# A hybrid decoder layer on one core: the last two value tiles of the attention go to other PSUM banks, and their last weight unit goes ahead of the first scores

## The chip, the cores and the metric

The kernel runs on one core of one Trainium2 chip. The metric is the device time of one execution in microseconds (us), the median of the runs shown. Besides those runs there is one execution under the hardware profiler, from which every row below comes.

The engines are named as in the profile: PE is TensorE (matmuls), PEld its weight loads, DVE VectorE, ACT ScalarE, POOL GpSimd, SP the engine that issues most transfers. Each works through its own instructions in their order.

## What is computed

One layer of a decoder for 512 tokens of width 1024, in float32:

```
u = RMSNorm(x);  z = u @ w_in          # q, k, v of attention | q, k, v, gates of an mLSTM | two branch gates
A = block-sparse causal attention      # 8 heads of 64, rotary on q and k, blocks of 256
B = chunked mLSTM                      # 4 heads of 128
m = sigmoid(gA) * (A @ w_proj_a) + sigmoid(gB) * (B @ w_proj_b)
x = x + m @ w_out
x = x + (silu(u2 @ w_gate) * (u2 @ w_up)) @ w_down,  u2 = RMSNorm(x);  then a last RMSNorm
```

The change touches only `z`'s columns for the attention's values (512 tokens by 512 columns, `va`) and what stands beside them in the program.

## The kernel before, in words

**Arithmetic.** Every float32 operand is split into a high and a low part (`split_hl`, line 157: ACT copies the high part, line 148; DVE subtracts it, line 161), and a product is three matmuls: high by high, low by high, high by low.

**Weight units.** The weights of the first half come in 60 units of 128x1024 float32, in the order of `UNITS` (line 68): q and k (six units), then `va` 0 to 3, then k 2 and 3, the output gate `ob` 0 and 1, and so on. `fill` (line 356) works off the next unit: it first splits units up to two ahead (`LOOK`), then calls the unit's generator up to its `yield`, calls `mid` if it was given one, and lets the generator finish. `split_unit` (line 189) takes two buffers of the kind W for each unit. There are ten of these; two are held by the parts of `u` for k 2 and 3 until all projections are done. The four `va` units hold the other eight until their last use, so unit 10 (k 2) can't be split before the `va` products let go of `va` 0's buffers. The raw weights go through buffers of the kind R, and the transfer of a later unit is issued on SP once a split has freed one.

**The values.** `run_v` (line 463) multiplies the four token tiles t = 0 to 3 (128 tokens each) with the four units. A unit holds two of the eight slices of the contraction. Tiles 0 and 1 are summed as the units arrive, in two banks of the kind `mm`. When the last unit is there, their sums are taken out by `evacuate` (ACT line 148 the high part, DVE line 487 the low part, two of each for a tile), and tiles 2 and 3 are multiplied in one go with all four units: 24 matmuls of 128x512 each (lines 470 to 472), in banks of the kind `mm`.

**PSUM.** Eight banks: three of the kind `mm` (all projections), three of the kind `S` (scores, transposes and the like), two of the kind `acc` (the attention's and the mLSTM's outputs, first used by `moba_c`, line 1309). A new tile of a kind waits until the bank that it takes has been read.

**The order of the work.** Up to `man.close()` the order is written out by hand. After it, a list scheduler fixes each engine's order when the program is built: its priority is the order in the program, and an instruction that isn't ready in its own estimate of the times lets later ones pass. On the chip, each engine then keeps that order. Around the change the program runs: unit q 3, `va` 0, the first gate rows (`gate_group(0)`), `va` 1, `va` 2, the mLSTM gates (`gates`, lines 1165 to 1187, a chain on DVE that ends with line 1184 and an ACT exponential), then the main loop. Step n of that loop traces the scores of one head and half (`moba_a`: lines 1219 to 1221 for the first 256 tokens, 1244 to 1246 for the others), then `fill(1, mid)` with one weight unit, then what had been put off (`later`, lines 1192 and 1193), and, some steps later, transposes (line 1290) and the products with the values (line 1309). At step 0 the scores are those of head 0, the unit is `va` 3, and `mid` runs between this unit's products for tiles 0 and 1 and their evacuation. The scores read stacks of k (`ks1`, `ks2`) that are gathered through DRAM by eight transfers of line 424, half of them issued on SP, half on POOL.

```
while n < len(steps) or qa or qb:
    ...
    r, second = moba_a(h, b) if kind == "a" else ml_a(h, b)
    ...
    fill(1, mid)
```

The second half of the layer (from about 400 us) is the gated feed-forward part with Strassen-like block sums, its order set by priorities from a plan of due times (`at`). The change does not touch it.

Of the kernel before, what the change touches and what calls it, by code (L numbers as in the profile page):

```python
# [84 lines left out]
def hybrid_layer_kernel(ctx: ExitStack, tc, xT, wall, wgu, wds, wdl, g3v, vecs, wgates, consts, rope, out):  # L85
# [13 lines left out]
    def nm(p="t"):  # L99
        cnt[0] += 1  # L100
        return f"{p}{cnt[0]}"
# [4 lines left out]
    def slot4(dt=F32, name="f"):  # L106
        return act.tile([P, 4, S], dt, name=nm(name), tag="A4", bufs=NA4)
# [8 lines left out]
    def mmb():  # L116
        return psum.tile([P, S], F32, name=nm("mm"), tag="mm", bufs=3)
# [4 lines left out]
    def accb():  # L122
        return psum.tile([P, S], F32, name=nm("acc"), tag="acc", bufs=2)
# [22 lines left out]
    def act_(out_, in_, func, **kw):  # L146
        if func not in SETS:
            return A.activation(out_, in_, func, **kw)  # L148
        table(SETS[func])
        if ph["manual"]:  # L150
            return A.activation(out_, in_, func, **kw)
        with tc.issue_after(ph["load"]):
            i = A.activation(out_, in_, func, **kw)
        ph["ins"].append(raw_ins(i))
        return i
# [33 lines left out]
    def split_unit():  # L189
        u = wstate["split"]  # L190
        wstate["split"] += 1
        whl[u] = split_hl(raw.pop(u), dst=(blk(F32R, "wh"), blk(F32R, "wl")))
        if u % 2 == 1:
            load_pair() if u < NGEN - 4 else st["load"]()
# [143 lines left out]
    def advance(n=1):  # L338
        for _ in range(n):
            while bulk:  # L340
                try:
                    next(bulk[0])
                    break
                except StopIteration:
                    bulk.pop(0)
# [5 lines left out]
    def add(g):  # L351
        bulk.append(g)
        return g


    def fill(n=1, mid=None):

        for _ in range(n):
            u = pos[0]
            if u >= len(UNITS):  # L360
                if mid:
                    mid()
                return
            while wstate["split"] <= min(u + LOOK, NGEN - 1):
                split_unit()
            pos[0] += 1
            kind, i = UNITS[u]
            g = run[kind](i, *whl.pop(u))
            next(g, None)
            if mid:  # L370
                mid()
            for _ in g:
                pass
# [89 lines left out]
    def run_v(kind):  # L463
        def products(ps, t, units):
            c = slice(t * P, (t + 1) * P)
            for j, (wh, wl) in units:
                for e in range(2):
                    k = 2 * j + e
                    h, l = wh[:, S * e : S * e + S], wl[:, S * e : S * e + S]
                    T.matmul(ps, uh[k][:, c], h, start=k == 0, stop=False)  # L470
                    T.matmul(ps, uh[k][:, c], l, start=False, stop=False)
                    T.matmul(ps, ul[k][:, c], h, start=False, stop=k == KT - 1)

        def evacuate(ps, t):
            c = slice(t * P, (t + 1) * P)
            for j in range(2):
                d = st[kind, j]
                o = ps[:, 256 * j : 256 * j + 256]
                if kind == "va":

                    o = o.rearrange("p (h d) -> p h d", h=4)
                    h, l = d[:, :, t * P : t * P + 64], d[:, :, t * P + 64 : (t + 1) * P]
                else:
                    o = o.rearrange("p (h d) -> p h d", h=2)
                    h, l = d[:, 0:4:2, c], d[:, 1:4:2, c]
                act_(h, o, AF.Copy, scale=rt[:, t : t + 1])
                V.scalar_tensor_tensor(l, o, rt[:, t : t + 1], f(h), op0=ALU.mult, op1=ALU.subtract)

        def fn(i, wh, wl):
            if i == 0:  # L490
                st[kind] = []
                st[kind, "ps"] = [mmb(), mmb()]
                for j in range(2):
                    d = st[kind, j] = slot4(F32R, kind)
                    if kind == "vb":
                        vml[2 * j], vml[2 * j + 1] = (d[:, 0, :], d[:, 1, :]), (d[:, 2, :], d[:, 3, :])
                    for e in range(4 if kind == "va" else 0):
                        vat[4 * j + e] = d[:, e, :]
            st[kind].append((i, (wh, wl)))
            for t in range(2):  # L500
                products(st[kind, "ps"][t], t, st[kind][-1:])
            yield
            if i == 3:
                for t in range(2):
                    evacuate(st[kind, "ps"][t], t)
                for t in range(2, 4):
                    ps = mmb()
                    products(ps, t, st[kind])
                    evacuate(ps, t)
        return fn  # L510
# [767 lines left out]
    def moba_b(h, b, prs):  # L1278

        res = []  # L1280
        for half in range(b + 1):
            pt = sb()
            n = 0
            for kk in range(2):
                kt = 2 * half + kk
                for t in range(2):
                    if kt > 2 * b + t:
                        continue
                    src = prs[0][:, P * (t + kt) : P * (t + kt + 1)] if b == 0 else prs[t][:, P * kt : P * kt + P]
                    T.transpose(pt[:, n : n + P], src, ident)  # L1290
                    n += P
            h_, l_ = slot(F32R, "pth"), slot(F32R, "ptl")
            res.append(split_hl(pt[:, :n], dst=(h_[:, :n], l_[:, :n])))
        return res
# [52 lines left out]
    def ml_a(h, b):  # L1347
        qh, ql = qkm[h]
        kh, kl = qkm[4 + h]
        res = []  # L1350
        for i in ((0, 1), (2,))[b]:
            ps = mmb() if i == 1 else sb()
            w = rbc[h][i]
            n = w.shape[-1]
            for j in range(4):
                if KR[j][0] == i:
                    c = slice(j * P, (j + 1) * P)
                    o = ps[:, KR[j][1]]
                    T.matmul(o, kh[:, c], qh[:, j * P :], start=True, stop=False)
                    T.matmul(o, kl[:, c], qh[:, j * P :], start=False, stop=False)  # L1360
                    T.matmul(o, kh[:, c], ql[:, j * P :], start=False, stop=True)
            V.scalar_tensor_tensor(w, ps[:, :n], sc_b, w, op0=ALU.mult, op1=ALU.mult)
            h_, l_ = slot(F32R, "Ah"), slot(F32R, "Al")
            res.append(split_hl(w, dst=(h_[:, :n], l_[:, :n])))

        w0, w1, w2 = rbc[h][0:3]
        if b == 0:
            V.tensor_tensor(w0[:, P:], w0[:, P:], w1, op=ALU.add)
        else:
            V.tensor_tensor(w0[:, 2 * P :], w0[:, 2 * P :], w2[:, 0:256], op=ALU.add)  # L1370
            V.tensor_tensor(w0[:, 3 * P :], w0[:, 3 * P :], w2[:, 256:384], op=ALU.add)
            res.append(split_hl(w0, "D"))
        return res, lambda: None
# [52 lines left out]
    for h in range(4):  # L1426
        for b in range(2):
            steps.append(("b", h, b))

    qa, qb = [], []  # L1430
    norms, norms_out = [], {}
    n = 0
# [10 lines left out]
    while n < len(steps) or qa or qb:  # L1443
        if qa and (len(qa) >= LA or n >= len(steps)):
            kind, h, b, r = qa.pop(0)
            qb.append((kind, h, b, moba_b(h, b, r) if kind == "a" else r, n))
        if n < len(steps):
            kind, h, b = steps[n]
            while kind == "b" and not (h in wready and h in qkm and 4 + h in qkm):
                advance()  # L1450
            r, second = moba_a(h, b) if kind == "a" else ml_a(h, b)
            qa.append((kind, h, b, r))
        else:
            second = lambda: None
        fl = list(pend)
        del pend[:]

        def mid():
            if n == 5:
                gate_group(1)  # L1460
            for g in todo.pop(n, ()):
                add(g)
            advance(2 if n < 13 else 3)
            second()

        fill(1, mid)
        for p_ in fl:
            p_()
        if norms:
            add(norm_d2(*norms.pop(0)))  # L1470
        while qb and (qb[0][4] <= n - LC):
            kind, h, b, r, _ = qb.pop(0)
            if kind == "a":
                moba_c(h, b, r)
            else:
                ml_c(h, b, r)
                if b == 1:
                    norms.append((h, ml_d1(h)))
        n += 1
# [106 lines left out]
```

## Time and profile before

| | |
|---|---|
| median of 3 runs | 759.62 us (758.28 to 760.0) |
| the profiled execution, its own time | 761.87 us |
| span in its profile, first to last instruction | 760.1 us |
| PE busy | 738.9 us (97%) |
| DVE busy | 624.0 us (82%) |
| ACT busy | 429.3 us (56%) |
| mean granted clock of PE | 0.991 |

A busy share is the time in which an engine had an instruction under way. "Idle before" is the time that the engine stood still ahead of an instruction, and the arrow names what ended that wait. Where an instruction waits for several things, the profile names the one that came last by its records, which can be a bystander. Matmuls overlap: one of 128x512 is shown with 0.39 us, while the next one starts 0.23 us after it.

### The profile page before, as it was taken

Reading aid. Unit: us, or ns where it says so; the run is one execution under the profiler, and the core shown is the slowest. Engines: PE = TensorE matmul, PEld = TensorE weight load, DVE = VectorE, ACT = ScalarE, POOL = GpSimd, SP = SyncE. Lnnn points to the kernel's source line nnn. Section 1 sums busy time; section 2 is a strip of 40 time slices with the busy share of each in tenths; the row PEclk is TensorE's granted clock in tenths of the full one; section 3 lists DMA queues with packets and bytes.
Section 4 is the critical chain, followed back from the end, with each engine's and each line's share of the span. In section 5 each row is a group of like instructions: output and inputs, shape, how many; then the busy total and the mean of one; then the engine's idle time right before and its main releaser. Section 6 shows DMA issues by size and latency. Waiting matters only on the chain. (4 is left out here: it accounts for less than half of the span.)

```text
span 760.1 us, 11421 instructions
## 1 busy us (share of the span) xinstructions
PE 738.9 (97%) x4230; PEld 639.0 (84%) x4230; DVE 624.0 (82%) x1065; ACT 429.3 (56%) x739; POOL 65.6 (9%) x82
## 2 busy tenths in 40 slices
PE   9998999999999999999999999989999999999994
PEld 5786888888888888888889997989899899899983
DVE  6896875889996787567688999878989988988996
ACT  7534666568765438523456566545745655665535
POOL 0002000000000000000000001300400400130003
PEclk9999999999999999999999999999999999999998
DMA  8776562432323213433676444962993795596402
GB/s 330 249 228 168 188 194 67 139 121 77 132 102 113 84 56 111 166 112 110 174 193 175 138 126 104 253 198 78 234 256 97 186 277 148 120 261 203 166 1 111
DMA packets 50839, 118.70 MB, mean 156 GB/s; under 512 B 4944, under 2 KB 9688, under 8 KB 50784
## 3 DMA queue, kind: packets, MB, share of 16 engines
q1 hardware_dynamic: 36832, 88.82, 34.7%
q0 software_dynamic: 9440, 26.77, 17.7%
q10 hardware_dynamic: 4512, 2.39, 1.0%
q8 instruction: 33, 0.54, 0.3%
q14 instruction: 22, 0.18, 0.1%
HBM read 101.16 MB, written 16.81 MB: 155 GB/s over the span
## 5 line engine op out<-in xcount | busy, mean ns | idle before, releaser
L148 ACT ACTIVATE wh<-raw 128x1024 fp32r<-128x1024 f32 x58 | 61.2, 1058 | 69.8 <-PE mm L202 63.0
L161 DVE TENSOR_TENSOR wl<-raw,wh 128x1024 fp32r<-128x1024 f32 x58 | 70.5, 1220 | 15.3 <-ACT wh L148 12.8
L783 PE MATMUL mm<-bq,w 128*128 128x256 f32 x264 | 77.0, 292 | 3.8 <-ACT s L148 3.3
L785 PE MATMUL mm<-bq,w 128*128 128x256 f32 x264 | 75.1, 284 | 0.0
L784 PE MATMUL mm<-bq,w 128*128 128x256 f32 x264 | 75.0, 284 | 0.0
L148 ACT ACTIVATE w<-s 128x1024 fp32r<-128x1024 f32 x44 | 46.6, 1060 | 45.7 <-DVE s L740 17.2
L731 DVE TENSOR_TENSOR w<-s,w 128x1024 fp32r<-128x1024 f32 x44 | 53.8, 1222 | 17.6 <-ACT w L148 15.8
L783 PEld LDWEIGHTS mm<-bq,w 128*128 128x128 f32 x264 | 50.7, 192 | 7.7 <-ACT s L148 5.4
L693 POOL DMA_DIRECT2D s<-in_wgu_dram x22 | 19.4, 882 | 413.8 <-DVE ga L585 127.8
L201 PE MATMUL mm<-u,wh 128*128 128x512 f32 x136 | 54.9, 403 | 0.0
L203 PE MATMUL mm<-u,wh 128*128 128x512 f32 x136 | 53.2, 391 | 0.0
L202 PE MATMUL mm<-u,wl 128*128 128x512 f32 x136 | 53.1, 390 | 0.0
L203 PE MATMUL mm<-ul,wh 128*128 128x512 f32 x136 | 52.9, 389 | 0.0
L201 PE MATMUL mm<-uh,wh 128*128 128x512 f32 x136 | 52.9, 389 | 0.0
L202 PE MATMUL mm<-uh,wl 128*128 128x512 f32 x136 | 52.9, 389 | 0.0
L148 ACT ACTIVATE w<-raw 128x1024 fp32r<-128x1024 f32 (+2 forms) x45 | 43.6, 974 | 15.4 <-PE s L784 9.2
L783 PE MATMUL s<-bq,w 128*128 128x256 f32 x176 | 50.3, 286 | 1.5 <-DVE gt L834 1.5
L784 PEld LDWEIGHTS mm<-bq,w 128*128 128x128 f32 x264 | 50.9, 193 | 0.1
L785 PEld LDWEIGHTS mm<-bq,w 128*128 128x128 f32 x264 | 50.9, 193 | 0.0
L785 PE MATMUL s<-bq,w 128*128 128x256 f32 x176 | 49.9, 283 | 0.0
L784 PE MATMUL s<-bq,w 128*128 128x256 f32 x176 | 49.7, 283 | 0.0
L148 ACT ACTIVATE w<-sw 128x1024 fp32r<-128x1024 f32 x20 | 21.2, 1060 | 31.2 <-DVE sw L770 29.4
(384 smaller groups left out, 2247.1 us busy)
## 6 DMA issues: line engine op xcount, KB each, us to landing
raw<-in_wall_dram SPq DMA_DIRECT2D x59, 512.0 KB, 3.4
s<-in_wgu_dram SPq DMA_DIRECT2D x22, 512.0 KB, 4.4
s<-in_wgu_dram POOLq DMA_DIRECT2D x22, 512.0 KB, 7.6
raw<-in_wgu_dram SPq DMA_DIRECT2D x22, 512.0 KB, 6.0
raw<-in_wds_dram SPq DMA_DIRECT2D x20, 512.0 KB, 7.1
w<-in_wgu_dram SPq DMA_DIRECT2D x22, 256.0 KB, 7.8
h1d<-s POOLq DMA_DIRECT2D x16, 256.0 KB, 12.4
R<-scr POOLq DMA_DIRECT2D x4, 896.0 KB, 4.8
```

Source lines behind the costliest of these rows:

```text
L148: return A.activation(out_, in_, func, **kw)
L161: V.tensor_tensor(l, src, f(h), op=ALU.subtract)
L201: T.matmul(ps, wh[:, c], rh[j], start=start and j == 0, stop=False)
L202: T.matmul(ps, wl[:, c], rh[j], start=False, stop=False)
L203: T.matmul(ps, wh[:, c], rl[j], start=False, stop=stop and j == n - 1)
L693: nc.gpsimd.dma_start(s13, wgu[i][:, 512:1536].rearrange("p (x c) -> p x c", x=2), accum_op=ALU.add)
L731: V.tensor_tensor(dst[1], src, f(dst[0]), op=ALU.subtract)
L783: T.matmul(ps, wh[:, c], bh, start=first and k == 0, stop=False, skip_group_check=not first)
L784: T.matmul(ps, wl[:, c], bh, start=False, stop=False, skip_group_check=not first)
L785: T.matmul(ps, wh[:, c], bl, start=False, stop=k == 3, skip_group_check=not first)
```

## The change

The sums of tiles 2 and 3 of the attention's values are put in the two banks of the kind `acc`, and a `fill(1)` ahead of the main loop takes the unit `va` 3; step 0 of the loop then takes none and calls only `mid`. All later steps take the same unit as before. The mLSTM's values (`vb`) keep their banks.

```
                 for t in range(2, 4):
-                    ps = mmb()
+                    ps = accb() if kind == "va" else mmb()
                     products(ps, t, st[kind])
                     evacuate(ps, t)
...
+    fill(1)
     qa, qb = [], []
     norms, norms_out = [], {}
     n = 0
...
-        fill(1, mid)
+        if n:
+            fill(1, mid)
+        else:
+            mid()
```

## Rows read from the trace of the kernel before

**Rows 1.** The page of the whole execution: busy time of each engine, then PE and its granted clock in 40 equal slices of 19 us (tenths).

```profile
PE 738.9 (97%) x4230; PEld 639.0 (84%) x4230; DVE 624.0 (82%) x1065; ACT 429.3 (56%) x739; POOL 65.6 (9%) x82
...
PE   9998999999999999999999999989999999999994
...
PEclk9999999999999999999999999999999999999998
```

**Rows 2.** Busy time in stretches: from and to in us, length, then PE, PEld, DVE, ACT, POOL (instructions), PE's granted clock, DMA share, GB/s.

```profile
62.50:73.30 10.80, 7.74 (x26) 5.67 (x25) 5.18 (x9) 4.93 (x8) 0.29 (x1) 0.84 0.40 105
...
80.00:460.00 380.00, 379.96 (x2021) 323.54 (x2020) 301.70 (x555) 222.40 (x413) 10.83 (x16) 1.00 0.41 127
460.00:740.00 280.00, 274.22 (x1856) 251.12 (x1855) 247.83 (x379) 157.43 (x236) 42.51 (x48) 0.99 0.67 175
```

**Rows 3.** Whom PE waited for over the whole execution: us in total, times, longest.

```profile
PE mm L783 <- ACT s L148: 3.3, 3, 2.1
PE mm L470 <- DVE va L487: 1.6, 1, 1.6
...
PE s L1219 <- DMA scr<-rr: 1.5, 1, 1.5
```

**Rows 4.** PE alone, in order of time, around 62 to 76 us: start, duration, line, operation, tiles, shape, and idle time before it with what ended it.

```profile
57.05 0.39 PE L470 MATMUL mm<-wh,u 128*128 128x512 f32 x1
...
62.27 0.39 PE L472 MATMUL mm<-wh,ul 128*128 128x512 f32 x1
64.22 0.47 PE L470 MATMUL mm<-wh,u 128*128 128x512 f32 x1 [1.57 <-DVE va L487]
66.18 0.30 PE L1219 MATMUL s<-ks,qs 128*128 128x128 f32 x1 [1.49 <-DMA scr<-rr]
66.32 0.44 PE L471 MATMUL mm<-wl,u 128*128 128x512 f32 x1
...
67.53 0.63 PE L472 MATMUL mm<-wh,u 128*128 128x512 f32 x1
67.96 0.63 PE L470 MATMUL mm<-wh,u 128*128 128x512 f32 x1
...
72.99 0.39 PE L472 MATMUL mm<-wh,ul 128*128 128x512 f32 x1
73.31 0.41 PE L1192 MATMUL s<-con,cr 4*128 4x4 f32 x4
73.65 0.44 PE L1244 MATMUL s<-ks,qs 128*128 128x384 f32 x1
73.93 0.40 PE L201 MATMUL mm<-u,wh 128*128 128x512 f32 x1
...
74.62 0.22 PE L1220 MATMUL s<-ks,qs 128*128 128x128 f32 x1
...
75.93 0.23 PE L1246 MATMUL s<-maskb,identb 128*128 128x128 bf16 x1
```

**Rows 5.** ACT, then DVE, in order of time from 60.9 us (columns as in rows 4).

```profile
61.38 0.63 ACT L153 ACTIVATE rr<-mr 4x512 f32<-4x512 f32 x1 [8.77 <-DVE mr L1184]
61.91 2.34 ACT L148 ACTIVATE va<-mm,rt 128x256 fp32r<-128x256 f32 x6
67.77 1.06 ACT L148 ACTIVATE wh<-raw 128x1024 fp32r<-128x1024 f32 x1 [3.51 <-PE mm L471]
70.33 1.06 ACT L148 ACTIVATE wh<-raw 128x1024 fp32r<-128x1024 f32 x1 [1.50 <-PE mm L471]
71.83 1.06 ACT L148 ACTIVATE wh<-raw 128x1024 fp32r<-128x1024 f32 x1 [0.45 <-PE mm L471]
...
60.93 0.41 DVE L1184 TENSOR_SCALAR mr<-mr 4x512 f32<-4x512 f32 x1
62.40 2.46 DVE L487 SCALAR_TENSOR_TENSOR va<-mm,rt,va 128x256 fp32r<-128x256 f32 x6 [1.06 <-ACT va L148]
68.86 1.23 DVE L161 TENSOR_TENSOR wl<-raw,wh 128x1024 fp32r<-128x1024 f32 x1 [4.00 <-ACT wh L148]
71.42 1.23 DVE L161 TENSOR_TENSOR wl<-raw,wh 128x1024 fp32r<-128x1024 f32 x1 [1.34 <-ACT wh L148]
72.92 1.23 DVE L161 TENSOR_TENSOR wl<-raw,wh 128x1024 fp32r<-128x1024 f32 x1 [0.28 <-ACT wh L148]
74.07 0.48 DVE L487 SCALAR_TENSOR_TENSOR va<-mm,rt,va 128x256 fp32r<-128x256 f32 x1
74.46 0.16 DVE L1193 COPY cS<-s 128x16 f32<-128x16 f32 x1
```

**Rows 6.** The tile of the k stacks between 50 and 70 us: who writes it, how often, duration in ns (least, median, greatest), first and last start in us; last, the time from issue to landing.

```profile
L424 SPq DMA_DIRECT2D ks<-sd x4: 303/376/448, 52.4 to 55.0; - x4
L424 POOL DMA_DIRECT2D ks<-sd x4: 550/550/555, 57.9 to 59.6; - x4
...
DMA to landing us min/median/max: 5.3/6.5/7.5
```

**Rows 7.** The tile of the attention's values over the whole execution (columns as in rows 6): the matmuls that read it and write a bank of the kind `acc`.

```profile
L1309 PE MATMUL acc<-pth,va x48: 222/278/283, 100.8 to 216.6; 128*128 128x256 f32 x32, 128*128 128x128 f32 x16
```

**Rows 8.** The page's list of the costliest groups: line, engine, operation, tiles, shape, count, then busy us, mean ns of one, idle time before them with what ended it.

```profile
L783 PE MATMUL mm<-bq,w 128*128 128x256 f32 x264 | 77.0, 292 | 3.8 <-ACT s L148 3.3
```

**Rows 9.** Stretches of 20 us (columns as in rows 2), from the attention and from the feed-forward part.

```profile
200.00:220.00 20.00, 20.00 (x106) 17.24 (x106) 19.37 (x34) 16.27 (x26) 0.00 (x0) 1.00 0.32 105
...
500.00:520.00 20.00, 17.92 (x135) 17.55 (x135) 15.00 (x28) 10.26 (x16) 0.88 (x1) 0.91 0.52 157
...
560.00:580.00 20.00, 18.50 (x150) 17.89 (x150) 16.55 (x29) 10.29 (x15) 0.88 (x1) 1.00 0.69 202
...
620.00:640.00 20.00, 19.18 (x156) 18.58 (x155) 17.22 (x30) 10.59 (x17) 0.89 (x1) 1.00 0.74 210
...
680.00:700.00 20.00, 19.26 (x155) 18.52 (x155) 17.20 (x32) 10.75 (x19) 0.88 (x1) 1.00 0.80 219
```

## The prediction

> **What bounds the kernel now.** The page comes first. PE is busy 738.9 us of a span of 760.1, DVE 624.0, ACT 429.3 [rows 1]: PE carries the time, and what can be gained without taking work from it is its 21 us of idle time and its slow clock. The 40 slices show where these are: one dip in the fourth slice (57 to 76 us), a smaller one about 510 us, the tail [rows 1]. The stretches make it exact [rows 2]. From 80 to 460 us PE idles 0.04 us of 380. From 62.5 to 73.3 us it is busy 7.74 of 10.80 us, and the granted clock is 0.84 on average. That is the one large loss in the first 460 us. The list of PE's waits names two of its kind: 1.6 us for DVE line 487 and 1.5 us at line 1219 [rows 3].
>
> PE's own instructions show how they follow each other [rows 4]. Token tile 2 runs from 57.05 to 62.50 without a gap: 23 steps from 57.05 to 62.27 are 0.227 us each. Tile 3 starts only at 64.22, released by DVE line 487: its `mm` bank is tile 0's, which is still being read. Why so late? ACT comes to the evacuation at 61.91, after the gates' exponential, which waited 8.77 us for DVE's chain [rows 5]. After a single product of tile 3, the first scores product (line 1219) stands next in PE's order. It waits until 66.18. The row names the write of `rr`, but line 1219 reads k and q stacks alone; the last k stacks were issued on POOL at 57.9 to 59.6 and took 5.3 to 7.5 us [rows 6], so the last lands between 64.9 and 67.1, and those of this product are among the earlier ones. Behind it stand 23 products of tile 3 that need nothing from it. Then the clock is down: line 472 at 67.53 and line 470 at 67.96 are 0.43 us apart, against 0.227, that is 1.2 in place of 2.4 GHz, after PE had done one product in about 3.7 us. Tile 3 ends at 72.99 + 0.23 = 73.22 [rows 4].
>
> **The change part by part.**
>
> *The stretch.* From 62.50 to 73.22 are 10.72 us. The work in it at full clock is 24 x 0.227 = 5.45 us, and 0.14 us for the scores product (66.18 to 66.32): 5.59 [rows 4]. The excess is **5.13 us**. As a check from other rows: idle 1.57 + 1.49 = 3.06, and (1 - 0.84) x 10.80 = 1.73 lost to the clock [rows 2, 4], together 4.79; the rest, 0.34, is starting up after each stop. The two kinds of bound are 4.8 and 5.1. The Trainium skill, page "TensorE: Matmul & The Clock Gate", section "Back-to-back issue gap", gives columns over 2.4 GHz plus 2.5 ns, 0.216 us for 512 columns; by it the work would be 5.32 and the excess 5.40. The trace's 0.227 is this kernel's own, and I take 5.13.
>
> *`acc` banks for tiles 2 and 3.* No sum of tile 3 waits for an evacuation any more. The banks are free: their first other user is line 1309 at 100.8 us [rows 7], and both new sums are read some 30 us before. A matmul costs no more there: 128x256 into `acc` has 278 ns in the median [rows 7], into `mm` a mean of 292 [rows 8]. This removes the wait of 1.57 us. Units k 2 and k 3 next need `mm` banks: one is now unused and two are released when the six evacuations end, at 64.25 on ACT and 64.86 on DVE [rows 5]. Nothing there is late.
>
> *The unit ahead of the scores.* The 24 products of tile 3 now have priority over line 1219, and all their operands are there. So PE should go from 62.27 straight on and end tile 3 at 62.50 + 5.45 = **67.95**. The scores come after. The last k stack lands by 59.6 + 7.5 = 67.1 at the latest [rows 6], 0.85 us earlier, so no wait is left at them. Is cover lost, since step 0 has no unit any more? Before, after 73.22, PE took the remaining scores of both halves between 73.65 and 75.97 with three products of k 2 between them [rows 4]: apart from one product, `va` 3 had already run. I cost this at nothing. The bound is the fourth bank of the kind `S`: two halves and line 1192 need four of three, and the fourth waits for DVE line 1193, which stands behind a split and an evacuation. If k 2 doesn't fill that, it is 1.2 us at most (69.6, worked out below, against scores that would want it near 68.4).
>
> *What is late next.* Unit k 2 needs W buffers, which `va` 0 gives back with tile 3's fifth and sixth product. ACT's first split started at 67.77, released by line 471 [rows 5]. Now the fifth ends at 63.6, and ACT is free at 64.25: split 64.25 to 65.31 on ACT, to 66.54 on DVE (1.06 and 1.23 us each). k 3 follows to 67.8, the next unit (17th and 18th product, 66.6) to 69.0; then tile 3's evacuation and line 1193, to 69.6. k 2's products are wanted at about 68.7, 2.1 us after its split. DVE ended its third split at 74.15 and will at 69.0: 5.15 earlier, just as much as PE. SP's raw loads are issued when a split has ended, and so move along; the DMA share here is 0.40 [rows 2]. `mid`'s work at step 0 (rotary of q, DVE) now stands behind the evacuations in the program; before, it ran behind them anyway.
>
> *Further on.* All that follows up to 460 us is PE's own pace, and DVE and ACT are shifted with it. I let the 5.1 us pass through whole. The feed-forward part stops four times at item boundaries, for 2.08, 1.50, 0.82 and 0.74 us [rows 9]; its loads are paced by buffers that PE's work frees, so they move too: nothing, with bounds of about 3.9 us both ways (the first stop's 2.08, and 0.09 x 20 = 1.8 by its clock).
>
> **Sum.** The profiled execution took 761.87 us (span 760.1, 1.8 around it): 761.87 - 5.13 = 756.7. It stands 2.25 us above the median of the runs shown, so the median should go from 759.62 to **754.5 us**. The runs shown differ by 1.7 us; about 0.2% (1.5 us) is what a measurement here can tell from no change.
>
> **The rivals.**
>
> *The scores still go first (no change).* The scheduler puts line 1219 ahead of most of tile 3, PE meets it at 62.5 and idles until 66.2, and the clock falls as before: 759.5. For: it did pass 23 products before, by its own estimate of when they and the stacks are ready. Against: then line 1219 had the higher priority, and now has the lower. 8%.
>
> *DVE takes a part (smaller gain).* The first split moves by only 67.77 - 64.25 = 3.5 us, since ACT is at the evacuations. If the chain of splits moves by that much and no more, 1.6 us of the gain come back as a wait at k 2 or later, where DVE has little air (19.37 of 20 us at 200 to 220 [rows 9]): 756.1. For: DVE is the second engine. Against: only the first split is held up; the third comes 5.15 us earlier. 9%. The Trainium skill, page "Perfetto Trace Analysis", section "Identifying the Most-Contended Engine", calls matmul busy time a poor measure of how near TensorE is to its limit, and weight-load time a better one; by it (323.54 of 380 us [rows 2]) PE would have 15% of air from 80 to 460 us, in which a gain made earlier could be lost. The trace speaks against that here: PE stands still for 0.04 us in that stretch, so it has no later wait to give the time to.
>
> *The feed-forward part gives it back (slower).* The stops at 560, 620 and 680 us last 1.50, 0.82 and 0.74 us and cost no clock; the one at 506 lasts 2.08 and takes the clock down to 0.91 over its 20 us [rows 9]. If the new order makes all three like the first, they cost 3 x 3.9 - 3.1 = 8.6 us more, less 5.1: 763.1. It decides once the part loses over 5.1 us more. For: DMA shares of 0.5 to 0.8 around the stops. Against: nothing there has an absolute time that the shift could run into. 7%.
>
> *One stop fewer there (larger gain).* The same reshuffle takes away the stop at 506: 754.5 - 3.9 = 750.6. 5%.
>
> **How the numbers follow.** The forecast has 66%; the rest, 5%, is for what I haven't named. The range takes in the forecast with 0.9 us of scatter and some 1.2 of new order in the feed-forward part (752.4 to 756.6), and the smaller gain with its scatter: up to 757.9. It leaves out the no-change case, the slower one and the larger gain, 20% in all. Faster by over 0.2% (below 758.1): 66 + 9 + 5 + 3 = 83%; within: 8 + 1 = 9%; slower: 7 + 1 = 8%.
>
> **What would show it.** Right: the 24 products of tile 3, into `acc`, directly behind those of tile 2, all 0.227 us apart; no row with idle time at lines 470 and 1219; granted clock 1.00 between 62 and 80; line 1219 at about 68; line 201 some 5 us before 73.93; 80 to 460 still without idle time, and the first feed-forward matmuls 5 us earlier. Wrong: line 1219 among tile 3's products with a wait before it; a wait at line 201 or 1244 for ACT or DVE; PE idle between 80 and 460; or stops in the feed-forward part that add up to over 5.1 us in sum.

## The result, and the profile after

The changed kernel took 755.48 us in the median of 10 runs (753.38 to 757.37), the kernel before 759.94 us in 10 runs beside it: a ratio of 0.9933, 95% interval 0.9918 to 0.9949. Two later comparisons gave 0.9935 (0.9920 to 0.9950) and 0.9934 (0.9913 to 0.9956). By these ratios that is 4.9 to 5.1 us, with intervals of 1.1 to 1.7 us to either side; the medians themselves lie 4.2 to 5.3 us apart, 4.5 in the first comparison. Forecast were 5.1 us, to 754.5, with a range from 752.4 to 757.9. The profiled execution took 755.47 us, with a span of 753.7.

PE alone, in order of time, in the changed kernel (columns as in rows 4; it answers to [rows 4]):

```profile
57.28 0.39 PE L470 MATMUL acc<-wh,u 128*128 128x512 f32 x1
...
62.49 0.39 PE L472 MATMUL acc<-wh,ul 128*128 128x512 f32 x1
62.72 0.39 PE L470 MATMUL acc<-wh,u 128*128 128x512 f32 x1
...
67.94 0.39 PE L472 MATMUL acc<-wh,ul 128*128 128x512 f32 x1
68.16 0.22 PE L1219 MATMUL s<-ks,qs 128*128 128x128 f32 x1
68.31 0.41 PE L1192 MATMUL s<-con,cr 4*128 4x4 f32 x4
68.65 0.44 PE L1244 MATMUL s<-ks,qs 128*128 128x384 f32 x1
68.93 0.39 PE L201 MATMUL mm<-u,wh 128*128 128x512 f32 x1
```

Tile 3 follows tile 2 after one step of 0.23 us; there is no idle time at lines 470 and 1219. From the start of tile 2 to line 1192 are 68.31 - 57.28 = 11.03 us; before they were 73.31 - 57.05 = 16.26 [rows 4]. (That is 5.23. About 0.1 us of it lies just ahead of line 1192: before, it follows the last 128x512 product by 0.32 us, where 0.23 is the usual step.) Busy time in stretches, changed kernel (columns and stretches as in [rows 2]):

```profile
62.50:73.30 10.80, 10.80 (x55) 8.88 (x53) 6.99 (x12) 6.80 (x12) 0.50 (x1) 1.00 0.68 170
...
80.00:460.00 380.00, 379.95 (x2025) 323.11 (x2024) 303.36 (x556) 221.14 (x411) 10.83 (x16) 1.00 0.41 128
460.00:740.00 280.00, 273.89 (x1851) 249.97 (x1850) 250.68 (x380) 160.23 (x243) 46.73 (x51) 1.00 0.67 175
```

The stretch is filled (10.80 of 10.80) at full clock, and behind it PE still has no idle time up to 460 us. So the gain has nowhere to be lost there, and it isn't. The products with the values (line 1309) and one group of the feed-forward matmuls (line 783, those that write a bank of the kind `mm` from `bq` and `w`) show it, the changed kernel's rows first, then the same line-783 row of the kernel before (columns as in rows 6: least, median, greatest duration, then first and last start):

```profile
L1309 PE MATMUL acc<-pth,va x48: 222/278/362, 96.2 to 211.7; 128*128 128x256 f32 x32, 128*128 128x128 f32 x16
...
L783 PE MATMUL mm<-bq,w x264: 277/283/502, 404.7 to 715.2; 128*128 128x256 f32 x132
```

```profile
L783 PE MATMUL mm<-bq,w x264: 278/283/502, 409.5 to 721.6; 128*128 128x256 f32 x132
```

The last of line 1309 comes 4.9 us earlier than in [rows 7], the first of this group of line 783 4.8 us earlier. As tile 2 began 0.23 us later in this execution (57.28 against 57.05), the stretch itself gave 5.0 to 5.1 us. The last of the group comes 6.4 us earlier: in the feed-forward part this pair of executions parts by another 1.6 us. The changed kernel's stretch there reads, beside [rows 9]:

```profile
500.00:520.00 20.00, 18.56 (x136) 17.54 (x137) 18.59 (x33) 11.49 (x19) 0.89 (x1) 1.00 0.34 93
```

PE idles 1.44 us in place of 2.08 (two stops, of 0.96 and 0.45 us, in place of one), and the clock is 1.00 in place of 0.91. The clock's share alone is 0.09 x 20 = 1.8 us. Whether that belongs to the change is what the repeats below ask.

ACT and DVE of the changed kernel (they answer to [rows 5]):

```profile
62.13 0.81 ACT L148 ACTIVATE va<-mm,rt 128x256 fp32r<-128x256 f32 x2
64.06 1.06 ACT L148 ACTIVATE wh<-raw 128x1024 fp32r<-128x1024 f32 x1 [1.12 <-PE acc L471]
...
65.15 1.23 DVE L161 TENSOR_TENSOR wl<-raw,wh 128x1024 fp32r<-128x1024 f32 x1 [1.66 <-ACT wh L148]
...
66.69 1.22 DVE L161 TENSOR_TENSOR wl<-raw,wh 128x1024 fp32r<-128x1024 f32 x1
...
69.27 0.17 DVE L1193 COPY cS<-s 128x16 f32<-128x16 f32 x1
...
70.29 1.22 DVE L161 TENSOR_TENSOR wl<-raw,wh 128x1024 fp32r<-128x1024 f32 x1
```

The first split starts when tile 3's fifth product lets go of its buffer, at 64.06, and is through at 66.38; the second at 67.91. They stand among the evacuations, not behind all of them. k 2's first product (line 201) ran at 68.93 with no idle time before it, so it waited for nothing.

### The profile page after: what moved, and what is told of

It reads as the page before. It is cut to its first block, busy times and chain, and to the rows that moved or that the text cites. A ratio compares the mean times of both kernels' runs of the same rounds, so it can differ in the third digit from the quotient of the medians.

```text
span 753.7 us, 11418 instructions
## 1 busy us (share of the span) xinstructions
PE 735.9 (98%) x4230; PEld 636.6 (84%) x4230; DVE 624.3 (83%) x1065; ACT 428.7 (57%) x739; POOL 65.5 (9%) x82
```

## The experiments

Three theories, as the expectations name them. A: the bank sets the start of tile 3, the scores cost what is left of the k stacks' transfer when PE comes to them, and the fall of the clock in the feed-forward part comes and goes. B: the change also takes away that fall. C: the scores' place ahead of tile 3's end has a price of its own, whatever the bank. A fourth, D, comes up where it is tested. Edits are shown against the kernel before, if nothing else is said.

**The two kernels again.** No edit, first the kernel before, then the changed one.

> The kernel before once more, unchanged, as a control on the same chip: how much its executions differ, and whether PE's clock falls in each of them at the stop in the feed-forward part (about 507 us), as it did in the profiled execution, or only in some. Every theory: ratio 1.000 within 0.002. Theory A (the stretch from 62.5 to 73.2 us is a fixed loss, the clock's fall at about 507 us comes and goes): PE again waits 1.6 us at line 470 and 1.5 us at line 1219, and ends token tile 3 at 73.2 +- 0.3 us; the time moves in steps of about 1.7 us with the number of falls of the clock. Theory B (the fall at 507 us belongs to the old order and the change takes it away too): half clock at about 507 us again, for 3.4 us.

> The changed kernel once more. Theory A: PE runs tile 3 behind tile 2 without a gap, ends it at 68.2 +- 0.3 us, its instructions behind 100 us come 4.8 to 5.1 us earlier than before, and the median is 4.5 to 5.5 us below that of before (ratio 0.993 to 0.994). Theory B: a second gain of 1.7 us in every execution at about 507 us, 6.4 us in all (ratio 0.9915).

Measured: 0.9994 (0.9977 to 1.0012) and 0.9935 (0.9920 to 0.9950). The stretches 500 to 520 us, first of the kernel before, then of the changed one:

```profile
500.00:520.00 20.00, 19.25 (x148) 18.23 (x147) 17.34 (x33) 10.43 (x17) 0.89 (x1) 1.00 0.53 157
```

```profile
500.00:520.00 20.00, 18.15 (x126) 17.49 (x127) 18.04 (x34) 10.77 (x18) 0.89 (x1) 0.91 0.36 93
```

This time it is the kernel before that keeps its clock (0.75 us idle) and the changed one that loses it (1.85 us idle). B falls: that fall goes with neither kernel. What is common to both pairs is the shift behind 100 us; the same group of line 783, first of the kernel before, then of the changed one:

```profile
L783 PE MATMUL mm<-bq,w x264: 277/283/501, 409.5 to 720.7; 128*128 128x256 f32 x132
```

```profile
L783 PE MATMUL mm<-bq,w x264: 276/283/501, 404.6 to 716.8; 128*128 128x256 f32 x132
```

The first comes 4.9 us earlier (4.8 in the first pair). The last comes only 3.9 us earlier, where it was 6.4: the feed-forward part gave 1.6 us in the first pair and took 1.0 in this one, so the 1.6 us were chance. In the stretch, theory A's rows are there again: the kernel before waits 1.57 and 1.50 us with a clock of 0.84 from 62.5 to 73.3 us, the changed one has no idle time and a clock of 1.00. Two details missed: the times of the kernel before (757.43 to 763.04 us) show no steps of 1.7 us, and the changed kernel's median lies 4.2 us below (forecast 4.5 to 5.5), though its ratio is as forecast.

**Only the banks.**

```
-                    ps = mmb()
+                    ps = accb() if kind == "va" else mmb()
```

> Only the banks are changed; the unit va 3 stays in step 0 of the loop, behind the first scores in the program. In this build's order for PE, line 1219 stands behind 15 of tile 3's 24 products. Theory A (the bank sets the start of tile 3, and the scores cost only what is left of the k stacks' transfer when PE comes to them): PE comes to line 1219 at about 62.5 + 15 x 0.227 = 65.9 us and waits 0.1 to 0.5 us; tile 3 ends at 68.0 to 68.7 us, the clock stays at 1.00, and the time is 4.3 to 5.1 us below before (ratio 0.993 to 0.9945): the move of the unit is worth under 0.7 us beside the banks. Theory C (the scores' place ahead of tile 3's end costs a wait of its own, whatever the bank): a wait of 1.5 us or more at line 1219, clock down, gain of only 1.6 to 2.5 us (ratio 0.997 to 0.998).

Measured: 0.9923 (0.9909 to 0.9937), median 755.55 us. PE around line 1219:

```profile
62.64 0.39 PE L472 MATMUL acc<-wh,ul 128*128 128x512 f32 x1
62.87 0.39 PE L470 MATMUL acc<-wh,u 128*128 128x512 f32 x1
...
66.04 0.39 PE L472 MATMUL acc<-wh,ul 128*128 128x512 f32 x1
66.81 0.30 PE L1219 MATMUL s<-ks,qs 128*128 128x128 f32 x1 [0.37 <-DMA scr<-rr]
66.94 0.44 PE L470 MATMUL acc<-wh,uh 128*128 128x512 f32 x1
...
68.83 0.39 PE L472 MATMUL acc<-wh,ul 128*128 128x512 f32 x1
69.15 0.41 PE L1192 MATMUL s<-con,cr 4*128 4x4 f32 x4
```

With a bank free, 15 products of tile 3 stand ahead of line 1219 in place of one, and fill nearly all of the time until the stacks land. 0.37 us of waiting is left. C falls for this build: the scores were traced ahead of tile 3's end and cost next to nothing. The time gained more than A had it (5.5 us by the medians, forecast 4.3 to 5.1). The stretch does not account for that: the group of line 783 starts at 405.5, 4.0 us earlier than before, and the second measurement below gives 0.9944.

Line 1219 waits for the stacks, and not for the write of `rr` that its rows name: the trace has the time at which each transfer landed and each wait ended. The scores need the first two of the four stacks' transfers from POOL. In the kernel before, the second of them lands at 65.88 us (issued at 58.49, 7.4 us to landing), and PE's wait for it ends at 65.91. With only the banks the two times are 66.40 and 66.43.

**Only the move.**

```
+    fill(1)
     qa, qb = [], []
...
-        fill(1, mid)
+        if n:
+            fill(1, mid)
+        else:
+            mid()
```

> Only the unit is moved; the sums of tiles 2 and 3 stay in banks of the kind mm. In this build's order for PE all 24 products of tile 3 stand ahead of line 1219. Theory A: tile 3 starts at 64.2 us as before (1.6 us of waiting for DVE line 487), runs without a further gap to 64.22 + 5.45 = 69.7 us; 3.4 us gained with the scores product, if the clock holds through the one stop of 1.6 us; 1.7 us if it falls (ratio 0.9955 or 0.9978). Theory C (the wait at line 1219 was the larger part and carries the fall of the clock): 3.4 us, clock 1.00. A rival to both (the banks carry all of it): under 1 us gained.

Measured: 0.9947 (0.9930 to 0.9964), median 757.36 us. PE's rows:

```profile
64.11 0.47 PE L470 MATMUL mm<-wh,u 128*128 128x512 f32 x1 [1.57 <-DVE va L487]
...
69.44 0.39 PE L472 MATMUL mm<-wh,ul 128*128 128x512 f32 x1
69.67 0.22 PE L1219 MATMUL s<-ks,qs 128*128 128x128 f32 x1
69.82 0.41 PE L1192 MATMUL s<-con,cr 4*128 4x4 f32 x4
```

The bank's wait stays, the scores' wait goes, and this one stop of 1.57 us didn't take the clock down (1.00 from 62.5 to 73.3). Line 1192 comes at 69.82, 3.5 us earlier than before (3.4 counted from the start of tile 2, which was 0.1 us earlier here), as A had it for a clock that holds. C forecast the same for this run, so it does not part the two; the rival that the banks carry all of it falls. The stretch:

```profile
62.50:73.30 10.80, 9.23 (x48) 7.35 (x48) 8.16 (x15) 6.73 (x11) 0.20 (x1) 1.00 0.58 173
```

**Banks, with the scores pinned ahead of tile 3.** The line with the banks is as in "Only the banks"; beside it:

```
-                    products(ps, t, st[kind])
+                    with ExitStack() as es:
+                        if kind == "va" and t == 3:
+                            es.enter_context(tc.issue_after(st["score"]))
+                        products(ps, t, st[kind])
...
-                T.matmul(o, qs[:, t * P : (t + 1) * P], k1[:, 0:n], start=True, stop=False)
+                i_ = T.matmul(o, qs[:, t * P : (t + 1) * P], k1[:, 0:n], start=True, stop=False)
+                st.setdefault("score", raw_ins(i_))
```

> The banks are changed as in the change, the unit is not moved, and tile 3's products are tied behind line 1219's first product in PE's order (an order only; nothing is computed differently). PE comes to line 1219 right after tile 2, at 62.5 us, and the k stacks land at about 66.1. Theory A (the wait for the stacks is an absolute time, and it costs what PE comes too early): one stop of 3.5 to 3.9 us at line 1219, then tile 3 without a gap to 66.2 + 0.1 + 5.45 = 71.8 us with the clock at 1.00, or 73.5 us if it falls for its 3.4 us; so 759.6 to 761.3 against 761.0 before, ratio 0.998 to 1.0005, and the gain of the banks is gone although no bank is waited for. Theory D (the bank alone carries the loss; the scores' place does not matter): as acc_only, ratio 0.992 to 0.9945.

Measured: 1.0005 (0.9987 to 1.0023). Line 1219 is line 1222 in this kernel. PE, then its stretch:

```profile
62.44 0.39 PE L472 MATMUL acc<-wh,ul 128*128 128x512 f32 x1
67.05 0.44 PE L1222 MATMUL s<-ks,qs 128*128 128x128 f32 x1 [4.22 <-DMA scr<-rr]
67.29 0.73 PE L470 MATMUL acc<-wh,u 128*128 128x512 f32 x1
67.83 0.63 PE L471 MATMUL acc<-wl,u 128*128 128x512 f32 x1
...
72.44 0.40 PE L471 MATMUL acc<-wl,uh 128*128 128x512 f32 x1
...
74.74 0.39 PE L472 MATMUL acc<-wh,ul 128*128 128x512 f32 x1
```

```profile
62.50:73.30 10.80, 6.58 (x20) 5.06 (x19) 3.71 (x8) 4.04 (x8) 0.48 (x1) 0.68 0.35 69
```

No bank is waited for, and the whole gain is gone: one stop of 4.22 us (forecast 3.5 to 3.9; the second transfer landed at 66.64, 0.8 us later than before, and the wait ended at 66.67) and a granted clock of 0.68. Tile 3 ends at 74.97, not at 71.8 or 73.5: A missed the size of the stop and the clock that followed it. In this profile the stretch costs even more than before (line 1192, now 1195, at 75.06 in place of 73.31); the times show no difference. So it is the time at which PE comes to the scores that counts. D, that the bank alone carries the loss, falls. Banks and order are two ways to the same thing: something for PE to do until about 66.5 us.

**One bank of the kind acc.** The edit is against the changed kernel.

```
-                    ps = accb() if kind == "va" else mmb()
+                    ps = accb() if kind == "va" and t == 2 else mmb()
```

> As the change, but only tile 2 goes to a bank of the kind acc; tile 3 takes the third mm bank, which is free. Theory A (it is the bank's being free that counts, not its kind): the same order on PE, no wait at lines 470 and 1219, tile 3 ends at 68.2 us, ratio 0.993 to 0.9945. A rival (mm has one bank too few for units k 2 and k 3 while tile 3 is summed): a wait of 0.5 us or more at lines 201 to 203 behind 68 us, ratio 0.995 or more.

Measured: 0.9938 (0.9916 to 0.9960). No wait at lines 470 and 1219, none at lines 201 to 203 behind 68 us:

```profile
68.12 0.22 PE L1219 MATMUL s<-ks,qs 128*128 128x128 f32 x1
68.28 0.41 PE L1192 MATMUL s<-con,cr 4*128 4x4 f32 x4
```

It is a free bank that tile 3 needs, not one of another kind.

**Is the move worth anything beside the banks?** The kernel with only the banks and the changed kernel once more, on one chip; no new edit.

> acc_only again, beside the changed kernel on one chip, to see whether the move of the unit is worth anything beside the banks. Theory A: in the stretch the move is worth 0.4 to 0.9 us (the wait left at line 1219), PE's instructions behind 100 us come 4.0 to 4.6 us earlier than before; in the time it is lost in the scatter of the feed-forward part: ratio 0.9920 to 0.9945. A rival (the move costs something later): again faster than the changed kernel by over 1 us.

> The changed kernel, beside acc_only_b. Theory A: PE's instructions behind 100 us come 4.8 to 5.1 us earlier than before, ratio 0.992 to 0.994, equal to acc_only_b within 0.8 us. The rival: over 1 us slower than acc_only_b.

Measured: banks alone 0.9944 (0.9922 to 0.9965), both 0.9934 (0.9913 to 0.9956), medians 756.1 and 755.3 us. In the first comparison it was the other way round (755.55 and 756.81). In the profile the wait at line 1219 is 0.38 us with the banks alone and nothing with both, and from the start of tile 2 to line 1192 are 11.73 us against 11.03. So the move is worth 0.7 us in the stretch, and no difference shows in the times. The rival, that the move costs something later, does not hold: the sign of the difference changed.

## Why the prediction was right

*What bounds the kernel.* Right. A gap of PE's at 62 us shifted everything behind it, by the same 4.8 to 4.9 us at 212 and at 405 us.

*The stretch, 5.13 us.* Right: 5.0 to 5.1 us. Tile 2 and 3 ran in 68.17 - 57.28 = 10.89 us, 48 x 0.227, so the trace's own step fits. The page "TensorE: Matmul & The Clock Gate" (section "Back-to-back issue gap") of the Trainium skill gives 0.216 us for one matmul of 512 columns by itself and 0.131 us in a stream of weight loads and matmuls; by an estimate from these the 48 products would have taken 10.4 or 6.3 us. The trace agrees with neither figure. One reading in the prediction's check is off: its rest of 0.34 us is not a start-up. The idle column counts from the shown end of a matmul, 0.39 us after its start, while the next could have started after 0.23. Counted from start to start [rows 4], the two stops cost 1.72 us (62.27 to 64.22) and 1.73 us (64.22 to 66.18) beyond a step, and the slow steps up to 73.22 cost 1.68: 5.13 in all, with nothing left over.

*Banks against move.* The prediction gave each part one of the two waits. That is too simple: the banks alone also do most of the second part's work, since the 15 products that could now run first cover the stacks' transfer (tile 2 began at 57.43; to line 1192 are 11.72 us, 4.5 less than before, where both parts together save 5.2), and the move alone gives 3.4, since with one wait less the clock holds. The parts add up to more than the whole.

*The scores come without a wait.* Right: line 1219 came at 68.16. All stacks had landed by 59.8 + 7.6 = 67.4 at the latest, by the changed kernel's rows of the k stacks:

```profile
L424 POOL DMA_DIRECT2D ks<-sd x4: 550/551/555, 58.2 to 59.8; - x4
...
DMA to landing us min/median/max: 5.3/6.5/7.6
```

The two transfers that line 1219 needs had landed by 66.23 (the second, issued at 58.72, took 7.5 us), so its margin was 1.9 us, not the 0.85 us of the prediction. The run with the pinned scores shows the other side of it.

*No cover lost at step 0.* Right: the fourth bank of the kind S held up nothing, k 2's products filled it.

*What is late next.* Right in its end, wrong in its working. I let the splits follow all six evacuations. In fact two evacuations ran, then splits and evacuations by turns; the first split waited 1.12 us on ACT for tile 3's fifth product, and the third ended at 71.51, not 69.0. PE waited for none of them.

*The rivals.* That the scores still go first did not happen, but it was a real possibility: pinned, it cost all of the gain. DVE took no part back: PE has 0.05 us of idle time from 80 to 460 us, although weight loads fill only 85% of it. The page "Perfetto Trace Analysis" of the Trainium skill (section "Identifying the Most-Contended Engine") takes weight-load time as one of the better measures of TensorE's headroom, and by it 15% would be left. The trace does not bear that out here: a gain made ahead of the stretch arrived behind it in full. The slower rival's stops in the feed-forward part did not grow in sum (the prediction took the idle time of each 20 us for one stop; its 1.50 at 560 us are two, of 0.96 and 0.45, its 0.82 two of 0.28 and 0.45): PE idles 6.11 us from 460 to 740 us, 5.78 before, and of the 6.11 some 0.7 are the last stop, which lay behind 740 us before.

*The larger gain.* In the first pair of profiles the stop at 506 us did cost less and the clock held; the repeat shows that this happens to either kernel, so it is chance.

## What to carry to other kernels

A short wait on the bounding engine can cost more than itself: two stops shown with 1.6 and 1.5 us took 5.1 us, by the slow clock behind them and by what the idle column leaves out, so sum the stretch, not the waits. Ask what else the engine could have done at that moment; if work that is ready stands behind the waiting instruction, a free buffer or another order gives most of the gain (here 4.5 or 3.4 of 5.2 us). And where the engine has no idle time afterwards, as here up to 460 us, a gain passes through whole; follow it by the start of the same instruction in both traces.

## What the runs showed that was not expected

**Both waits go back to one chain.** ACT came late to the evacuation because its exponential waited 8.77 us for DVE's chain of the mLSTM gates [rows 5]. The k stacks were late for the same reason, which the prediction did not see. In the kernel before, POOL's transfers of the stacks stand behind a write of `rr`, which waits for that chain:

```profile
57.42 0.54 POOL L1187 DMA_DIRECT2D scr<-rr  x1 [8.14 <-DVE rr L1182]
57.95 2.18 POOL L424 DMA_DIRECT2D ks<-sd  x4
```

What the first two of the four read had been in DRAM since 53.99 us, and SP issued its own half from 52.4 to 55.0 [rows 6]. Issued at 54.0, with the 6.9 to 7.4 us to landing that they took, they would be there by about 61.9, ahead of tile 2's end at 62.5. That is an estimate; no run tried another order on POOL.

**The clock.** One stop of 1.57 us left the clock at 1.00 (only the move); two of 1.57 and 1.49 us with one product between them had it at half for 3.4 us (0.84 over 10.8 us); with one of 4.22 us it fell while PE still stood, and was at half from 65.0 to 71.8 us (0.68 over 10.8 us). About 500 to 520 us it fell in the two executions with a single stop of 2.08 and 2.00 us, and in none of the other eight. The idle time summed over these 20 us does not tell the cases apart: the run with the pinned scores had 1.88 us there, in stops of 1.40 and 0.44, and kept its clock, where the changed kernel's second execution lost it with 1.85.

```profile
500.00:520.00 20.00, 18.12 (x147) 17.51 (x146) 16.23 (x29) 10.33 (x18) 0.89 (x1) 1.00 0.60 175
```

**The scatter.** Most of the scatter of the kernel before goes with the clock. Beside the second set of experiments its 21 executions lay between 757.32 us at a mean granted clock of 0.996 and 763.81 us at 0.988, with a correlation of -0.9 between time and clock. The difference of 0.008 is about 6 us of 760. Where the clock fell in these executions is not on record. The fastest of them is only some 2 us above the changed kernel's median of 755.3. What sets the length of the stop in the feed-forward part was not tried and stays open.
